# A wait at the shared port: GpSimd's port operations wait by semaphore for the VectorE operation that the plan put ahead of them

## The chip, the cores and the metric

The kernel runs on one core of one Trainium2 chip. The metric is the device time of one launch in microseconds (us), lower is better. Before the change three runs took 1005.16, 1011.17 and 1012.47 us (median 1011.17).

## The reference, cut to what matters

The reference is a two-layer encoder trunk on 256 tokens of width 1024, all in float32. Each layer is a SwiGLU FFN (width 2816), a mixer, and a second SwiGLU FFN, each between two RMS norms:

```
x = x + 0.5 * rmsnorm(swiglu(rmsnorm(x, g0), wg0, wu0, wd0), g1)
m = mixer(rmsnorm(x, g2));  x = x + rmsnorm(m, g3)
x = x + 0.5 * rmsnorm(swiglu(rmsnorm(x, g4), wg1, wu1, wd1), g5)
```

The mixer of layer 0 (the even mixer) projects to nine parts, turns queries and keys by rotary tables (RoPE), runs four differential attention heads and eight heads whose keys are selected by an indexer (the 64 best keys of each query), and projects the result back. The mixer of layer 1 is a chunked band attention with a relative bias. Only the even mixer has work for GpSimd at the port that this change is about.

## The kernel before, in words

**Tiling.** Tokens stand in two tiles of 128 rows. Every product of two float32 matrices is made of three products of rounded parts: a tile is split into a high part (a cast) and a low part (the tile less the high part), and TensorE adds high by high, high by low and low by high. For weights this is done by `Unit.start` (from L250 on): SyncE loads a 512 KB piece of the weights into a staging buffer `raw` (L269, 6 such buffers), ScalarE casts it to `wh` (L277) in pieces of 128x512, and the low part `wl` is one subtraction per piece (L279, `lo`), which reads `raw` and `wh`, both in SBUF. There are 8 buffers each for `wh` and `wl`.

**Which engine makes the low parts.** In the FFNs and in layer 1 it is VectorE (DVE). In the even mixer the units `ua[1]` to `ua[5]` and `uo` are made with `pool=True`: the subtraction may then go to VectorE or to GpSimd (POOL), to whichever the plan finds free first. The same holds for the sum at the end of `rope` (L744): a tile `t` plus a tile `t`, both in SBUF, of 512 or 288 columns. What `rope` does ahead of it (L736, L740) reads PSUM and stays on VectorE. The transposes of a rope's result on TensorE are L427.

**The plan sets the order.** All operations are first written into a list (`Plan.op`), with an estimated duration, a place in the order (`pos`) and the operations that they depend on. `Plan.issue` (L93) then runs a small event simulation with one clock per engine, and calls each operation's function when the simulated engine takes it; that fixes the order of the instructions on every engine. On the chip each engine works through its own row in order, and waits by semaphores for data and buffers alone.

**The port in the plan.** Operations that are marked `port=True` are held to use one port that VectorE and GpSimd share: while one of them runs in the simulation (until `port`, set when it is taken), no other marked operation of the two engines is taken. Nothing of this reaches the chip: there, the two engines meet at the port as their own waits let them.

Of the kernel before, what the change touches and what calls it, by code (L numbers as in the profile page):

```python
# [52 lines left out]
class Plan:  # L53
# [36 lines left out]
        self.pos += us  # L90
        return self.last

    def issue(self):  # L93
        free = dict(SLOTS)
        eng = {e: 0.6 for e in LAT}
        heap = {e: [] for e in LAT}
        ev, n, port = [], 0, 0.0
        todo = len(self.ops)

        def push(o):  # L100
            for e in o["eng"]:
                heapq.heappush(heap[e], (o["pos"], o["id"], o))

        def event(t, kind, x):
            nonlocal n
            n += 1
            heapq.heappush(ev, (t, n, kind, x))

        for o in self.ops:
            if o["n"] == 0:  # L110
                push(o)
        event(0.6, "", None)
        now = 0.0
        while ev:
            now = ev[0][0]
            while ev and ev[0][0] <= now + 1e-9:
                _, _, kind, x = heapq.heappop(ev)
                if kind == "ready":
                    push(x)
                elif kind == "free":  # L120
                    free[x.tag] += x.n
            for e in heap:
                if eng[e] > now + 1e-9:
                    continue
                skip, got, late = [], None, None
                while heap[e]:
                    z = heapq.heappop(heap[e])
                    o = z[2]
                    if o["end"] is not None:
                        continue  # L130
                    need = [q for q in o["refs"] if q.t is None]
                    fits = all(free[q.tag] >= sum(p.n for p in need if p.tag == q.tag) for q in need)

                    if o["port"] and e != "ACT" and port > now + 1e-9:
                        fits = False
                        event(port, "", None)
                    for q in o["refs"]:

                        if q.tag in BANKS and q.used[0] != e and q.used[1] > now + 1e-9:
                            fits = False  # L140
                            event(q.used[1], "", None)
                    if fits and o["safe"] <= now + 1e-9:
                        got = o
                        break
                    if fits and late is None:
                        late = z
                    skip.append(z)
                if got is None and late is not None:
                    got = late[2]
                    skip.remove(late)  # L150
                for z in skip:
                    heapq.heappush(heap[e], z)
                if got is None:
                    continue
                o = got
                need = [q for q in o["refs"] if q.t is None]
                for q in need:
                    free[q.tag] -= q.n
                    q.t = q.make()
                us = o["us"] if len(o["eng"]) == 1 else o["us"][e]  # L160
                o["fn"]() if len(o["eng"]) == 1 else o["fn"](e)
                if o["port"] and e != "ACT":
                    port = now + us
                end = eng[e] = o["end"] = now + us
                todo -= 1
                event(end, "", None)
                for q in o["refs"]:
                    q.used = (e, end + 0.1)
                for d in o["out"]:
                    d["n"] -= 1  # L170
                    at = end + (OWN[e] if d["eng"] == (e,) else o["lat"])
                    d["ready"] = max(d["ready"], at)
                    if d["eng"] == ("PE",) != (e,):
                        d["safe"] = max(d["safe"], at + SAFE)
                    if d["n"] == 0:
                        d["ready"] = max(d["ready"], now)
                        event(d["ready"], "ready", d)
                for q in o["refs"]:
                    q.left -= 1
                    if q.left == 0:  # L180
                        event(end + 0.05, "free", q)
        assert todo == 0, [(o["eng"], o["pos"], o["n"], [q.tag for q in o["refs"]])
                           for o in self.ops if o["end"] is None][:20]
        return now
# [11 lines left out]
def trunk_kernel(  # L196
# [25 lines left out]
    pl = Plan()  # L222
    op, main = pl.op, pl.main
    PE, ACT, DVE, POOL, DMA = ("PE",), ("ACT",), ("DVE",), ("POOL",), ("DMA",)
# [895 lines left out]
    for l in range(2):  # L1120
        for p in range(3):
# [11 lines left out]
            else:  # L1133
                ffn(l, p // 2, xT, nxt)
            xT = z
    pl.issue()


# [48 lines left out]
```

## Time and profile before

| what | value |
| --- | --- |
| median of three runs | 1011.17 us |
| the three runs | 1005.16, 1011.17, 1012.47 us |
| the profiled execution, time | 1006.86 us |
| its span on the core | 1005.1 us |
| busy in the span: TensorE (PE) | 991.6 us, 99% |
| busy: VectorE (DVE) | 725.7 us, 72% |
| busy: ScalarE (ACT) | 607.4 us, 60% |
| busy: GpSimd (POOL) | 85.2 us, 8%, 107 instructions |
| TensorE's granted clock, mean | 0.999 of full speed |

The profile is one execution, so its rows add up to its own span of 1005.1 us, and some 1.8 us lie around it in the 1006.86 us. Rows of a timeline give the start from the span's beginning, the time of one or of several merged instructions (x5 is five of them), the engine, the line of the kernel, and in square brackets how long the engine had been idle and what ended it. An instruction that stands at the port is shown as busy: it has started, and lasts longer.

### The profile page before, as it was taken

How to read it: one execution, taken by the hardware profiler on the slowest of the kernel's cores; microseconds unless marked ns; L12 is line 12 of the kernel's file. 1: busy time of each engine (PE TensorE's matmuls, PEld its weight loads, DVE VectorE, ACT ScalarE, POOL GpSimd, SP SyncE). 2: the span in 40 equal slices, each digit the busy share in tenths (PEclk: the TensorE clock that was granted, in tenths of full speed). 3: DMA queues.
4: the chain of work that ended last, by engine and by line, in shares of the span. 5: the costliest groups of instructions: out<-in, count | busy, mean ns of one | idle time of the engine just before them, and what ended most of it. 6: DMA issues, size and time to landing. Idle time of an engine off the chain costs nothing.

```text
span 1005.1 us, 15484 instructions
## 1 busy us (share of the span) xinstructions
PE 991.6 (99%) x5435; PEld 847.6 (84%) x5435; DVE 725.7 (72%) x1537; ACT 607.4 (60%) x1376; POOL 85.2 (8%) x107
## 2 busy tenths in 40 slices
PE   9999999999999999999999999999999999999997
PEld 8888888877888988888888888888888888888886
DVE  7766668689888676677577667676778877666682
ACT  8555556556588555565466555576578856555661
POOL 1000000156531100000020000001100010000000
PEclk9999999999999999999999999999999999999999
DMA  9866665555545567666467666664775447666621
GB/s 343 293 184 178 196 191 144 161 178 167 167 138 157 166 218 200 192 187 190 146 209 247 180 182 192 195 178 149 224 267 159 124 148 251 188 179 194 192 87 42
DMA packets 125933, 185.52 MB, mean 185 GB/s; under 512 B 6040, under 2 KB 93984, under 8 KB 125856
## 3 DMA queue, kind: packets, MB, share of 16 engines
q1 hardware_dynamic: 125856, 184.54, 59.9%
q8 instruction: 42, 0.69, 0.3%
q14 instruction: 35, 0.29, 0.1%
HBM read 183.47 MB, written 1.05 MB: 184 GB/s over the span
## 4 chain that ended last, share of the span: by engine, by line
PE 89%; DVE 7%; ACT 2%; issue 1%; DMA 1%; POOLq 0%; DVEq 0%; ACTq 0%; POOL 0%
PE ps L387 26%; PE ps L389 14%; PE y L417 9%; PE y L418 9%; PE y L419 9%; PE ps L412 4%; PE ps L409 4%; PE ps L410 4%; PE ps L427 2%; DVE wl L279 2%; PE ps L417 2%; PE ps L418 2%; PE ps L419 2%; PE ps L795 1%; DMA g<-in_norm_g_dram 1%
## 5 line engine op out<-in xcount | busy, mean ns | idle before, releaser
L279 DVE TENSOR_TENSOR wl<-raw,wh 128x512 fp32r<-128x512 f32 (+2 forms) x636 | 418.0, 689 | 133.5 <-ACT wh L277 91.3
L277 ACT CAST wh<-raw 128x512 fp32r<-128x512 f32 (+2 forms) x668 | 378.8, 615 | 124.5 <-issue 70.1
L387 PE MATMUL ps<-xT,wh 128*128 128x512 f32 x1152 | 290.4, 393 | 0.0
L387 PEld LDWEIGHTS ps<-xT,wh 128*128 128x128 f32 x1152 | 208.1, 189 | 38.0
L389 PEld LDWEIGHTS ps<-xT,wl 128*128 128x128 f32 x1152 | 157.5, 190 | 11.6
L389 PE MATMUL ps<-xT,wl 128*128 128x256 f32 x1152 | 162.8, 283 | 0.0
L417 PE MATMUL y<-wh,blk 128*128 128x512 f32 x352 | 138.1, 392 | 0.0
L418 PE MATMUL y<-wl,blk 128*128 128x512 f32 x352 | 137.4, 390 | 0.0
L419 PE MATMUL y<-wh,blk 128*128 128x512 f32 x352 | 137.1, 390 | 0.0
L409 PE MATMUL ps<-wh,xT 128*128 128x512 f32 (+2 forms) x320 | 107.6, 351 | 0.1
L410 PE MATMUL ps<-wl,xT 128*128 128x512 f32 (+2 forms) x320 | 106.1, 347 | 0.8 <-DVE wl L279 0.3
L396 DVE TENSOR_TENSOR t<-ps,t 128x256 f32<-128x256 f32 x144 | 60.6, 421 | 44.3 <-ACT t L395 42.8
L395 ACT COPY t<-ps 128x256 f32<-128x256 f32 x144 | 53.6, 373 | 51.8 <-PE ps L389 48.0
L453 POOL TENSOR_TENSOR sm<-sm 128x1 f32<-128x1 f32 x24 | 14.9, 621 | 777.9 <-ACT t L534 721.4
L419 PEld LDWEIGHTS y<-wh,blk 128*128 128x128 f32 x352 | 66.1, 188 | 13.9
L417 PEld LDWEIGHTS y<-wh,blk 128*128 128x128 f32 x352 | 66.2, 188 | 12.8
L418 PEld LDWEIGHTS y<-wl,blk 128*128 128x128 f32 x352 | 66.2, 188 | 12.6
L410 PEld LDWEIGHTS ps<-wl,xT 128*128 128x128 f32 x320 | 60.6, 189 | 8.8 <-DVE wl L279 2.3
L412 PE MATMUL ps<-wh,xT 128*128 128x512 f32 (+2 forms) x320 | 67.6, 347 | 0.0
L409 PEld LDWEIGHTS ps<-wh,xT 128*128 128x128 f32 x320 | 60.5, 189 | 8.0 <-ACT xT L363 0.5
L680 ACT ACTIVATE t<-t 128x256 f32<-128x256 f32 x64 | 26.8, 418 | 55.2 <-DVE t L679 55.2
L412 PEld LDWEIGHTS ps<-wh,xT 128*128 128x128 f32 x320 | 51.3, 189 | 6.6
(148 smaller groups left out, 1030.7 us busy)
## 6 DMA issues: line engine op xcount, KB each, us to landing
raw<-in_wd_dram SPq DMA_DIRECT2D x88, 512.0 KB, 4.2
raw<-in_wg_dram SPq DMA_DIRECT2D x86, 512.0 KB, 4.4
raw<-in_wu_dram SPq DMA_DIRECT2D x86, 512.0 KB, 4.5
raw<-in_ew_in_dram SPq DMA_DIRECT2D x24, 512.0 KB, 4.6
raw<-in_ow_in_dram SPq DMA_DIRECT2D x24, 512.0 KB, 4.5
g<-in_norm_g_dram SPq DMA_DIRECT2D x11, 512.0 KB, 5.7
raw<-in_ew_out_dram SPq DMA_DIRECT2D x8, 512.0 KB, 3.7
raw<-in_ow_out_dram SPq DMA_DIRECT2D x8, 512.0 KB, 4.0
```

The source lines that it names most:

```text
L277: nc.scalar.copy(ref.t[0][:, sl], raw.t[:, sl])
L279: (nc.vector if e == "DVE" else nc.gpsimd).tensor_sub(ref.t[1][:, sl], raw.t[:, sl], ref.t[0][:, sl].bitcast(F32))
L387: nc.tensor.matmul(b.t, w()[0], xT.both[:, k].rearrange("p j c -> p (j c)"), start=k == 0, stop=False)
L389: nc.tensor.matmul(b.t[:, 0:S], w()[1], xT.t[0][:, k, :], start=False, stop=k == KT - 1)
L395: op(ACT, n_act(S, True), lambda: nc.scalar.copy(dst.t[:, sl], b.t[:, S:512]), r=[b], w=[(dst, sl.start)])
L396: op(DVE, n_dve(S), lambda: nc.vector.tensor_add(dst.t[:, sl], b.t[:, 0:S], dst.t[:, sl]), r=[b], w=[(dst, sl.start)])
L409: nc.tensor.matmul(o(), ah, bh, start=k == 0, stop=False)
L410: nc.tensor.matmul(o(), ah, bl, start=False, stop=False)
L412: nc.tensor.matmul(o(), al, bh, start=False, stop=k == KT - 1)
L417: nc.tensor.matmul(o, ah, bh, start=start, stop=False)
L418: nc.tensor.matmul(o, ah, bl, start=False, stop=False)
L419: nc.tensor.matmul(o, al, bh, start=False, stop=stop)
```

## The change

`issue` now gets the tile context `tc`. In the simulation it remembers in `held` the last VectorE operation that was taken at the port, and to each GpSimd operation taken at the port it adds a dependency on that one, of the kind that becomes a semaphore wait on the chip. The wait goes one way: VectorE's operations get none for GpSimd's.

```diff
-    def issue(self):
+    def issue(self, tc):
...
-        ev, n, port = [], 0, 0.0
+        ev, n, port, held = [], 0, 0.0, None
...
                 if o["port"] and e != "ACT":
                     port = now + us
+
+                    done = tc.nc.cur_bb.bb.instructions[-1]
+                    if e == "DVE":
+                        held = done
+                    elif held is not None:
+                        tc.add_manual_dep(done, held.name, mybir.DependencyInfo(mybir.DependencyClass.Sync, mybir.DependencyReason.DATA),
+                                          reason="port")
...
-    pl.issue()
+    pl.issue(tc)
```

The order of the instructions stays the same on all five engines; what changes is what some of them wait for. The first two pieces are GpSimd's row in the even mixer, from its second rope sum on: `t` are the two tiles of that sum, `wl`, `wh` and `raw` the low part, the high part and the staging buffer of a weight piece, and the names in brackets are the semaphores waited for. Before:

```order
27 L744 TENSOR_TENSOR t_360_2196<-t_360_2196,t_361_2202 128x512 [waits DVE_49,PE_49]
28 L279 TENSOR_TENSOR wl_2225<-raw_2036,wh_2224 128x512 [waits DMAHW0_49,Activation_49]
29 L279 TENSOR_TENSOR wl_2252<-raw_2084,wh_2251 128x512 [waits DMAHW3_49,PE_49,Activation_49]
30 L279 TENSOR_TENSOR wl_2263<-raw_2129,wh_2262 128x512 [waits DMAHW5_49,PE_49,Activation_49]
31 L744 TENSOR_TENSOR t_370_2240<-t_370_2240,t_371_2245 128x288 [waits DVE_49]
32 L894 COPY t_370_2240<-t_370_2240 128x96 [waits Pool_49]
33 L279 TENSOR_TENSOR wl_2319<-raw_2275,wh_2318 128x512 [waits DMAHW1_49,Activation_49]
```

And GpSimd's row at the same place with the change (its lines are seven further down in the file):

```order
27 L751 TENSOR_TENSOR t_360_2196<-t_360_2196,t_361_2202 128x512 [waits DVE_49,PE_49]
28 L286 TENSOR_TENSOR wl_2225<-raw_2036,wh_2224 128x512 [waits DMAHW0_49,Activation_49]
29 L286 TENSOR_TENSOR wl_2252<-raw_2084,wh_2251 128x512 [waits DVE_49,DMAHW3_49,PE_49,Activation_49]
30 L286 TENSOR_TENSOR wl_2263<-raw_2129,wh_2262 128x512 [waits DMAHW5_49,PE_49,Activation_49]
31 L751 TENSOR_TENSOR t_370_2240<-t_370_2240,t_371_2245 128x288
32 L901 COPY t_370_2240<-t_370_2240 128x96 [waits Pool_49]
33 L286 TENSOR_TENSOR wl_2319<-raw_2275,wh_2318 128x512 [waits DMAHW1_49,DVE_49,Activation_49]
```

Two subtractions (29 and 33) have gained a wait for VectorE; the sum in 31 has lost its own, which the wait in 29 covers, since GpSimd works in order. The sum in 27 names the same semaphore as before, but the value waited for is higher by one instruction: it stands for the second multiplication of L529 now, and for the rope's L740 before. Of GpSimd's 32 subtractions nine have gained a wait in this way: each is the first of a run of GpSimd operations that follows port work on VectorE in the plan.

SyncE's row changes too. The pieces below are its loads of staging buffers at the time of those GpSimd operations. Before:

```order
98 L269 DMA raw_2312<-in_ew_in_dram 128x2x512 [waits DMAHW3_49,DVE_49,Pool_49]
99 L269 DMA raw_2328<-in_ew_in_dram 128x2x512 [waits DMAHW4_49,DMAHW5_49,DVE_49,Pool_49]
100 L269 DMA raw_2360<-in_ew_in_dram 128x2x512 [waits DMAHW7_49,DVE_49]
101 L269 DMA raw_2375<-in_ew_in_dram 128x2x512 [waits DMAHW1_49,DMAHW6_49,Activation_49,Pool_49]
102 L269 DMA raw_2430<-in_ew_in_dram 128x2x512 [waits DMAHW0_49,DVE_49]
```

With the change the same five loads read:

```order
98 L276 DMA raw_2312<-in_ew_in_dram 128x2x512 [waits DMAHW3_49,Pool_49]
99 L276 DMA raw_2328<-in_ew_in_dram 128x2x512 [waits DMAHW4_49,DMAHW5_49,DVE_49,Pool_49]
100 L276 DMA raw_2360<-in_ew_in_dram 128x2x512 [waits DMAHW7_49,DVE_49]
101 L276 DMA raw_2375<-in_ew_in_dram 128x2x512 [waits DMAHW6_49,DMAHW0_49,DVE_49]
102 L276 DMA raw_2430<-in_ew_in_dram 128x2x512 [waits DMAHW1_49,Activation_49,Pool_49]
```

The loads 101 and 102 have changed staging buffers: the buffer that GpSimd frees is now taken by the later of the two, the one that VectorE frees by the earlier.

## Rows read from the trace of the kernel before

**Rows 1.** The page's first part: busy time of the engines in the whole span, share of the span, instructions.
```profile
PE 991.6 (99%) x5435; PEld 847.6 (84%) x5435; DVE 725.7 (72%) x1537; ACT 607.4 (60%) x1376; POOL 85.2 (8%) x107
```

**Rows 2.** Busy time by stretch of the span (us from its start): length, then busy us of each engine with its instructions, granted clock, share of the DMA engines, GB/s.
```profile
0.00:10.00 10.00, 8.29 (x38) 6.82 (x38) 4.52 (x17) 6.18 (x19) 0.69 (x6) 1.00 0.77 244
...
200.00:310.00 110.00, 105.86 (x639) 86.25 (x638) 96.54 (x272) 72.50 (x193) 53.83 (x43) 1.00 0.51 157
310.00:995.00 685.00, 684.06 (x3732) 588.00 (x3732) 487.94 (x985) 412.31 (x913) 23.11 (x42) 1.00 0.60 183
995.00:1005.07 10.07, 3.57 (x16) 2.63 (x14) 3.00 (x6) 1.38 (x4) 0.74 (x2) 0.87 0.15 53
```

**Rows 3.** The same view, two pieces of 10 us out of the even mixer.
```profile
210.00:220.00 10.00, 9.48 (x44) 7.20 (x42) 9.97 (x15) 7.33 (x14) 8.72 (x8) 1.00 0.52 143
220.00:230.00 10.00, 7.81 (x55) 6.06 (x55) 9.82 (x16) 3.21 (x9) 2.85 (x3) 1.00 0.64 219
```

**Rows 4.** Waits of TensorE's matmuls between 200 and 310 us: who waited for whom, us in total, times, the longest.
```profile
PE ps L427 <- DVE t L744: 2.5, 2, 1.7
PE ps L427 <- DVE pt L369: 0.7, 1, 0.7
PE ps L427 <- POOL t L744: 0.5, 1, 0.5
```

**Rows 5.** Timeline of TensorE, pieces between 210 and 231 us.
```profile
210.84 0.66 PE L427 MATMUL ps<-ident,t 128*128 128x128 f32 x4 [0.52 <-POOL t L744]
...
213.64 1.98 PE L412 MATMUL ps<-wh,xT 128*128 128x512 f32 x8
...
219.51 0.49 PE L427 MATMUL ps<-ident,t 128*128 128x128 f32 x3
221.67 0.63 PE L427 MATMUL ps<-ident,t 128*128 128x128 f32 x4 [1.67 <-DVE t L744]
...
230.35 0.63 PE L427 MATMUL ps<-ident,t 128*128 128x128 f32 x4 [0.87 <-DVE t L744]
```

**Rows 6.** Timeline of GpSimd between 203 and 224 us.
```profile
204.37 0.81 POOL L744 TENSOR_TENSOR t<-t,t 128x288 f32<-128x288 f32 x1 [2.05 <-DVE t L740]
...
209.19 1.60 POOL L744 TENSOR_TENSOR t<-t,t 128x512 f32<-128x512 f32 x1 [3.69 <-DVE t L740]
210.75 1.29 POOL L279 TENSOR_TENSOR wl<-raw,wh 128x512 fp32r<-128x512 f32 x1
212.72 3.32 POOL L279 TENSOR_TENSOR wl<-raw,wh 128x512 fp32r<-128x512 f32 x2 [0.68 <-ACT wh L277]
216.00 1.24 POOL L744 TENSOR_TENSOR t<-t,t 128x288 f32<-128x288 f32 x1
217.31 0.61 POOL L894 COPY t<-t 128x96 f32<-128x96 f32 x1
217.89 1.29 POOL L279 TENSOR_TENSOR wl<-raw,wh 128x512 fp32r<-128x512 f32 x1
219.71 2.94 POOL L279 TENSOR_TENSOR wl<-raw,wh 128x512 fp32r<-128x512 f32 x2 [0.54 <-ACT wh L277]
```

**Rows 7.** Timeline of VectorE, pieces between 208 and 231 us.
```profile
208.17 0.87 DVE L740 SCALAR_TENSOR_TENSOR t<-ps,sm,r 128x256 f32<-128x256 f32 x2
208.96 0.68 DVE L529 TENSOR_TENSOR blk<-X,g 128x512 f32<-128x512 f32 x1
...
211.13 6.67 DVE L279 TENSOR_TENSOR wl<-raw,wh 128x512 fp32r<-128x512 f32 x5
217.72 0.68 DVE L371 SCALAR_TENSOR_TENSOR blk<-ps,blk 128x512 fp32r<-128x512 f32 x1
218.32 0.73 DVE L736 SCALAR_TENSOR_TENSOR t<-ps,sm,r 128x512 f32<-128x512 f32 x1
218.98 0.86 DVE L740 SCALAR_TENSOR_TENSOR t<-ps,sm,r 128x256 f32<-128x256 f32 x2
219.88 1.65 DVE L744 TENSOR_TENSOR t<-t,t 128x512 f32<-128x512 f32 x1
221.45 3.56 DVE L279 TENSOR_TENSOR wl<-raw,wh 128x512 fp32r<-128x512 f32 x4
...
229.52 0.69 DVE L744 TENSOR_TENSOR t<-t,t 128x512 f32<-128x512 f32 x1
```

**Rows 8.** Groups of instructions: VectorE's subtractions between 200 and 310 us; the columns are line, engine, operation, tiles, shapes, count, then busy us, mean ns of one, idle us ahead of them with what ended it.
```profile
L279 DVE TENSOR_TENSOR wl<-raw,wh 128x512 fp32r<-128x512 f32 x27 | 23.1, 896 | 2.4 <-ACT wh L277 2.3
```

**Rows 9.** The same group between 310 and 990 us, where GpSimd makes no low parts.
```profile
L279 DVE TENSOR_TENSOR wl<-raw,wh 128x512 fp32r<-128x512 f32 x458 | 300.2, 686 | 100.2 <-ACT wh L277 68.3 <-PE ps L389 30.9
```

**Rows 10.** GpSimd's instructions that write or read `wl`: duration in ns, shortest, median and longest, first and last start in us.
```profile
L279 POOL TENSOR_TENSOR wl<-raw,wh x32: 1264/1292/2551, 210.7 to 302.2; 128x512 fp32r<-128x512 f32 x32
```

**Rows 11.** Timelines at two later places: GpSimd's subtractions at 261 and 284 us.
```profile
261.09 2.55 POOL L279 TENSOR_TENSOR wl<-raw,wh 128x512 fp32r<-128x512 f32 x1 [4.95 <-ACT wh L277]
...
284.14 1.76 POOL L279 TENSOR_TENSOR wl<-raw,wh 128x512 fp32r<-128x512 f32 x1 [1.14 <-ACT wh L277]
```

**Rows 12.** VectorE at the same two places.
```profile
260.61 0.69 DVE L744 TENSOR_TENSOR t<-t,t 128x512 f32<-128x512 f32 x1
261.21 1.29 DVE L279 TENSOR_TENSOR wl<-raw,wh 128x512 fp32r<-128x512 f32 x2
...
283.47 3.58 DVE L279 TENSOR_TENSOR wl<-raw,wh 128x512 fp32r<-128x512 f32 x4
```

## The prediction

> **What bounds the kernel now.** The first view is the busy time of the engines: TensorE is busy 991.6 of 1005.1 us, GpSimd 85.2 [rows 1]. The kernel's time is TensorE's work plus the 13.5 us in which it stands. The second view, busy time by stretch, says where it stands: 1.7 us in the first 10 us, 6.5 us in the last 10, 0.9 us in the 685 us from 310 on, and 110.00 - 105.86 = 4.14 us between 200 and 310 us [rows 2]. That is the even mixer, the only place where GpSimd makes low parts. No edit at the port can give back more than these 4.14 us, unless TensorE's own work got shorter, and the change leaves its instructions and their order as they are.
>
> The third view names what TensorE waits for there: 2.5 us in two waits for VectorE's rope sums and 0.5 us in one wait for GpSimd's rope sum [rows 4]; the timeline puts them at 210.84 (0.52 us), 221.67 (1.67 us) and 230.35 (0.87 us) [rows 5]. VectorE is busy 9.97 and 9.82 of 10 us just there [rows 3], but part of that is standing at the port. A subtraction takes it 686 ns where GpSimd is quiet [rows 9] and 896 ns on average between 200 and 310 us [rows 8]; 27 x 0.21 = 5.7 us are lost so. It can be seen in single rows: from 211.13 five subtractions take 6.67 us, while GpSimd works beside them, and the rope sum at 219.88 takes 1.65 us, while GpSimd runs two subtractions from 219.71 [rows 6, 7]. At 261 two of VectorE's subtractions with no GpSimd operation ahead of them take 1.29 us, a step of 0.60 us each and 0.69 for the last [rows 12].
>
> GpSimd stands as well: its subtractions take 1.29 us in the median and 2.55 us at the longest [rows 10]. Where one stands, it ends a fixed time after the other's operation: VectorE's run of five ends at 217.80, which is 0.56 us after GpSimd's sum ended (216.00 + 1.24) [rows 6, 7]; GpSimd's sum of 209.19 ends at 210.79, 1.15 us after VectorE's L529 ended (208.96 + 0.68).
>
> On the first of these I weighed a rule of the Trainium skill. SBUF — State Buffer, "Who interferes with whom", says that a VectorE operation with two SBUF inputs and a GpSimd operation that reads SBUF exclude each other for a whole instruction, and that whoever issues first gets the port. The rows at 211 to 218 us agree. Those at 261 do not agree in the second half: GpSimd's subtraction started at 261.09, yet the two of VectorE that followed, from 261.21 on, went ahead unstretched, and GpSimd ended at 263.64 [rows 11, 12]. By the rule the port's total time stays what it is and a wait only chooses who stands; what that gives is the first rival below.
>
> **The change part by part.** It adds nine waits to GpSimd's subtractions and raises the value of one that a rope sum already had. No instruction is added to VectorE, TensorE or ScalarE. A wait matters only where the named VectorE operation ends after GpSimd would have started.
>
> *First place, 209 us.* GpSimd's rope sum (27 in its order) must now wait for L529, which ends at 209.64. It already stood for it at the port and ended at 210.79 [rows 6, 7]. Semaphore to start is 0.15 us (L740 ended at 209.04, the sum started at 209.19), a clean operation 1.29 us: it would end at 209.64 + 0.15 + 1.29 = 211.08. TensorE waits for it at 210.84 already [rows 5], so this costs 0.3 us.
>
> *Second place, 212 us.* Subtraction 29 started at 212.72; now it waits for the last of VectorE's five subtractions, which ended at 217.80: 5.08 us late if nothing else moved. But VectorE's run gets shorter. Its first still stands behind GpSimd's 28 (ends 212.04, plus 0.56 = 212.60), the other four take 0.60 each: 215.00, which is 2.8 us earlier. GpSimd then starts at 215.15 and its two subtractions end at 215.15 + 2 x 1.29 = 217.73, where they ended at 216.04. VectorE meanwhile does L371, L736 and L740, which read PSUM; L736 needs TensorE's products, done at 213.64 + 1.98 = 215.62 [rows 5], so its rope sum L744 is asked for at 215.66 + 0.66 + 0.80 = 217.1, stands until 217.73, and ends at 218.3 in place of 221.53. GpSimd's small sum (31; 0.81 us clean [rows 6]) comes behind it and ends at 218.3 + 0.66 = 219.0, the copy (32; 0.26 to 0.61) at 219.2 to 219.6. Queued behind the wait are thus 30, 31 and 32, and TensorE waits for 32 at 219.51 [rows 5]: 0 to 0.2 us late. The next transposes, which stood 1.67 us for L744, stand no more. Gain: 1.67 - 0.2 = 1.5 us.
>
> *Third place, 218 us.* Subtraction 33 (started 217.89) now waits for VectorE's four subtractions from 221.45. These come after L744 and GpSimd's small sum, the first ending near 219.5, the last near 221.3 (before: 225.01). GpSimd's three then run from 221.45 to 225.3, where they ended at 222.65. They are 2.7 us late. No wait of TensorE for a GpSimd low part is among [rows 4]; what waits for them is SyncE, for a staging buffer. There the exchange of buffers helps: load 101 no longer waits for GpSimd, load 102 does. I cost this at nothing; the cover is the slack of loads and casts ahead of the products, and without it the price is 2.7 us. That is below the second rival's and does not come on top of it: a TensorE that is late at the second place wants these parts later by as much.
>
> *Fourth place, 230 us.* TensorE stands 0.87 us for VectorE's L744 of 229.52. VectorE's backlog ahead of it has become 3.7 us shorter (225.01 against 221.3), TensorE's products that feed L736 come 1.2 us earlier. The wait can go fully or not at all; I take half, 0.4 us.
>
> *The others.* At 261 GpSimd stood until VectorE was done (2.55 us instead of 1.29), so the wait only makes standing into waiting: 0. At 284 it will start 1.3 us later and VectorE's run of four (3.58 us; clean 3 x 0.60 + 0.69 = 2.5) gets 1.1 us shorter [rows 11, 12]; no wait of TensorE in [rows 4] is for either: 0.
>
> *Sum:* +0.3 - 1.5 - 0.4 = -1.6 us. Ends: -4.1 us if every wait of TensorE in this stretch goes, +3.1 us if the second place turns against TensorE (second rival). I take the sum, since its largest term rests on a single row that shows both the stretch and the wait. What is late next after L744 is the copy 32. The profiled execution took 1006.86 us, so it would take 1005.3; it lies 4.3 us below the median of the three runs, and on that the forecast is 1011.17 - 1.6 = 1009.6 us.
>
> **The rivals.**
>
> *The port's time is only shared out anew.* VectorE gets no wait for GpSimd, so GpSimd's late operations meet later VectorE operations, as L744 at the second place does. Then VectorE's 5.7 us come back elsewhere, TensorE's waits move, and the net is the 0.3 us of the first place: 1011.5 us. For it: the longest stretches are not all covered by a wait (VectorE's first subtraction at 211.13 stays behind GpSimd's 28, which has none). Against it: between 221 and 231 us VectorE works on PSUM for the most part, where GpSimd costs it nothing, as L371, L736 and L740 of 217.72 to 219.84 show, at 0.43 to 0.73 us each beside a busy GpSimd [rows 6, 7]. The rule of the Trainium skill's page SBUF — State Buffer, named above, is for this rival.
>
> *Slower: GpSimd's late copy makes TensorE stand.* Place: the transposes at 219.51. They have 2.26 us after the end of the small sum at 217.24, and 1.6 us after that of the copy (217.92). If VectorE's five subtractions do not get shorter, GpSimd is released at 217.80, 5.08 us late; by the slack of the small sum 5.08 - 2.26 = 2.8 us reach TensorE, and with the first place's 0.3 it is +3.1: 1014.3 us. It decides from the point at which VectorE's run ends after 216.6 (215.0 plus the copy's slack). For it: VectorE's run depends on casts of ScalarE too. Against it: VectorE shows no idle between 211.13 and 219.88.
>
> *The change does not do what it says.* The waits are there in GpSimd's order, but one-way; if at the port VectorE mostly goes ahead anyway, as at 261, they say only what happens already: 0, that is 1011.2 us.
>
> **How the numbers follow.** The forecast (a gain of 1 to 4 us) gets 0.50, sharing anew 0.22, no effect 0.10, slower by 1 us or more 0.18. All four lie within 1% (10 us), which is about what a measurement of this kernel can tell from no change: the three runs already span 7.3 us. Beyond 1% on either side there is only the spread of runs or a mechanism that I don't see: 0.04 each, 0.92 for the same. The range takes the ends on the lowest and the highest run: 1005.16 - 4.1 = 1001.0 and 1012.47 + 3.1 = 1015.6. The forecast's own is 1007 to 1010.
>
> **What would show it.** Right: VectorE's five subtractions at 211 take near 3.9 us (212.60 - 211.13 = 1.5, and 4 x 0.60) and its L744 behind them 0.7 to 1.2; the wait of 1.67 us is gone; GpSimd waits for VectorE near 213 and 219 us; TensorE's busy time between 200 and 310 us nearer to the stretch's length. Wrong: a wait of TensorE for GpSimd's copy or sum of over 1 us, VectorE's mean in rows 8 still near 896 ns, or TensorE waiting for casts whose load stood behind GpSimd.

## The result, and the profile after

The change takes 1003.73 us (median of 7 runs, 1001.74 to 1005.65); the kernel before, run beside it, 1009.98 us (7 runs, 1005.16 to 1012.47). The ratio is 0.9943, with a 95% interval from 0.9920 to 0.9966: 0.57% faster, 6.25 us between the medians. The prediction was 1009.6 us and a gain of 1.6 us: inside 1%, as most of its chance said, and inside the wide range of 1001.0 to 1015.6, but below the forecast's own 1007 to 1010 us, and the gain is four times as large.

The profiled execution of the change took 1003.96 us, its span is 1002.2 us, 2.9 us shorter than that of before. First the busy times of the whole span:

```profile
PE 991.6 (99%) x5435; PEld 847.9 (85%) x5435; DVE 721.9 (72%) x1537; ACT 607.4 (61%) x1376; POOL 82.5 (8%) x107
```

TensorE has the same work as in [rows 1]. VectorE and GpSimd are "busy" 3.8 and 2.7 us less with the same instructions: that was standing at the port. In the timelines and groups below a line of the kernel stands seven further down than before (L279 is L286, L744 is L751, L427 is L434). The stretch from 200 to 310 us, columns as in [rows 2]:

```profile
200.00:310.00 110.00, 108.39 (x652) 88.61 (x651) 94.84 (x279) 75.18 (x200) 50.28 (x43) 1.00 0.51 161
```

TensorE stands 110.00 - 108.39 = 1.61 us there, against 4.14. Its waits in this stretch, to set beside [rows 4]:

```profile
PE ps L434 <- DVE pt L376: 0.7, 1, 0.7
PE ps L434 <- POOL t L751: 0.6, 1, 0.6
PE ps L802 <- DVE blk L378: 0.3, 1, 0.3
```

The two waits for VectorE's rope sums, 2.5 us, are gone. The columns are who waited for whom, us in total, times and the longest, as there. Now GpSimd's timeline, to set beside [rows 6]:

```profile
209.55 1.29 POOL L751 TENSOR_TENSOR t<-t,t 128x512 f32<-128x512 f32 x1 [4.07 <-DMA raw<-in_ew_in_dram]
210.79 1.30 POOL L286 TENSOR_TENSOR wl<-raw,wh 128x512 fp32r<-128x512 f32 x1
215.27 2.55 POOL L286 TENSOR_TENSOR wl<-raw,wh 128x512 fp32r<-128x512 f32 x2 [3.18 <-PE ps L419]
217.77 1.27 POOL L751 TENSOR_TENSOR t<-t,t 128x288 f32<-128x288 f32 x1
219.10 0.61 POOL L901 COPY t<-t 128x96 f32<-128x96 f32 x1
221.59 3.79 POOL L286 TENSOR_TENSOR wl<-raw,wh 128x512 fp32r<-128x512 f32 x3 [1.88 <-ACT blk L372]
```

And VectorE's operations that meet it, to set beside [rows 7]:

```profile
210.90 4.14 DVE L286 TENSOR_TENSOR wl<-raw,wh 128x512 fp32r<-128x512 f32 x5
...
217.27 1.10 DVE L751 TENSOR_TENSOR t<-t,t 128x512 f32<-128x512 f32 x1
218.29 3.16 DVE L286 TENSOR_TENSOR wl<-raw,wh 128x512 fp32r<-128x512 f32 x4
...
225.97 0.68 DVE L751 TENSOR_TENSOR t<-t,t 128x512 f32<-128x512 f32 x1
```

GpSimd starts its pair at 215.27, 0.23 us after VectorE's five end (210.90 + 4.14 = 215.04), and its three at 221.59, 0.14 us after the four end (218.29 + 3.16 = 221.45). The releasers printed there, PE and ACT, are only the last semaphore event that the profile sees; the ends of VectorE's rows tell what was waited for. VectorE's five take 4.14 us in place of 6.67, the four 3.16 in place of 3.56, and its second rope sum comes at 225.97 in place of 229.52. GpSimd's pair starts 2.55 us late and its three end at 225.38 in place of 222.65, and no wait of TensorE for a low part of GpSimd appears. In the same group between 200 and 310 us the mean of a subtraction on VectorE falls from the 896 ns of [rows 8] to

```profile
L286 DVE TENSOR_TENSOR wl<-raw,wh 128x512 fp32r<-128x512 f32 x28 | 19.8, 745 | 2.4 <-ACT wh L284 2.3
```

Between these two profiled executions the gain is 2.9 us, 2.5 of them in this stretch. The other 3.4 us of the 6.25 are the question that the experiments answer.

### The profile page after: what moved, and what is told of

The parts are those of the page before. It is cut to its first block, busy times and chain, and to the rows that moved or that the text cites. A ratio compares the mean times of both kernels' runs of the same rounds, so it can differ in the third digit from the quotient of the medians.

```text
span 1002.2 us, 15484 instructions
## 1 busy us (share of the span) xinstructions
PE 991.6 (99%) x5435; PEld 847.9 (85%) x5435; DVE 721.9 (72%) x1537; ACT 607.4 (61%) x1376; POOL 82.5 (8%) x107
## 4 chain that ended last, share of the span: by engine, by line
PE 92%; DVE 4%; ACT 1%; DMA 1%; issue 1%; SPq 0%; POOL 0%; POOLq 0%; DVEq 0%; ACTq 0%
PE ps L394 26%; PE ps L396 14%; PE y L424 9%; PE y L425 9%; PE y L426 9%; PE ps L416 5%; PE ps L419 5%; PE ps L417 5%; PE ps L434 3%; PE ps L426 2%; PE ps L425 2%; PE ps L424 2%; PE ps L802 1%; DVE wl L286 1%; DMA g<-in_norm_g_dram 1%
## 5 line engine op out<-in xcount | busy, mean ns | idle before, releaser
L286 DVE TENSOR_TENSOR wl<-raw,wh 128x512 fp32r<-128x512 f32 (+2 forms) x636 | 414.1, 683 | 133.8 <-ACT wh L284 89.7
```

The source lines that it names most:

```text
L286: (nc.vector if e == "DVE" else nc.gpsimd).tensor_sub(ref.t[1][:, sl], raw.t[:, sl], ref.t[0][:, sl].bitcast(F32))
```

## The experiments

All runs below were taken in three groups; the median of before in them is 1009.5 (23 runs), 1009.01 (23) and 1008.64 us (18). Ratios are to the kernel before, in the same group, with 95% intervals. In the edits `nth` counts GpSimd's port operations in the plan's order; the line that counts them is not shown, and it moves the later lines of the kernel down by one more (L279 is L287, L744 is L752, L427 is L435).

### What does before usually look like? (again, again2: the kernel before, unchanged)

> The kernel before once more, nothing changed, for a second profiled execution and more times. Theory A (lottery at the port): without the waits the order at the port is settled anew in each execution by small shifts, so executions of the same program stand differently long in the even mixer; the times spread from 1005 to 1012 us with a median near 1010, and in the new profile TensorE stands for another time between 200 and 310 us than the 4.14 us of the first profile, while the stretches outside agree within 0.5 us. Theory B (elsewhere): what lies between the first profile (1006.86 us) and the median (1009.98) is loading or start-up, so TensorE stands for 4.1 us again between 200 and 310 us and the difference shows in other stretches. Theory C (chance): the true time of before is near 1006.9 us and the gain is the 2.9 us of the two profiles; the median here is then 1007 us or less.

1009.84 us (1005.38 to 1011.31, 12 runs), ratio 1.0000 (0.9987 to 1.0014). The profiled execution took 1010.72 us, with a span of 1008.7 us, 3.6 more than the profile that the prediction was made from. Its page, the first line:

```profile
PE 993.0 (98%) x5435; PEld 848.4 (84%) x5435; DVE 728.5 (72%) x1537; ACT 607.7 (60%) x1376; POOL 87.2 (9%) x107
```

TensorE's same work takes 1.4 us more than in [rows 1]. The stretch:

```profile
200.00:310.00 110.00, 103.75 (x612) 84.03 (x610) 96.00 (x260) 70.31 (x186) 54.91 (x43) 0.98 0.50 156
```

TensorE stands 6.25 us there and not 4.14, and its granted clock is 0.98 in the mean. 2.1 + 1.4 = 3.5 us: that is the difference of 3.6 us but for 0.1 us. TensorE's timeline shows the place; compare the last line of [rows 5]:

```profile
232.67 1.09 PE L427 MATMUL ps<-ident,t 128*128 128x128 f32 x4 [3.96 <-DVE t L744]
233.41 2.05 PE L412 MATMUL ps<-wh,xT 128*128 128x512 f32 x4
```

It stands 3.96 us for the rope sum for which it stood 0.87 us in the first profile. The granted clock, the third figure from the end, in the 2 us in which the stand ends (at 232.67), and in the 2 after these:

```profile
232.00:234.00 2.00, 1.33 (x6) 1.27 (x7) 1.83 (x5) 0.21 (x1) 1.65 (x1) 0.50 0.88 255
234.00:236.00 2.00, 2.00 (x24) 1.25 (x26) 1.46 (x6) 1.41 (x3) 0.00 (x0) 0.64 0.57 139
```

0.50 is the lower of the two levels, 1.2 GHz: four transposes take 1.09 us in place of 0.63. The reason for the stand is on VectorE:

```profile
220.65 4.68 DVE L279 TENSOR_TENSOR wl<-raw,wh 128x512 fp32r<-128x512 f32 x4
...
229.23 1.62 DVE L279 TENSOR_TENSOR wl<-raw,wh 128x512 fp32r<-128x512 f32 x1
230.78 1.75 DVE L744 TENSOR_TENSOR t<-t,t 128x512 f32<-128x512 f32 x1
```

and GpSimd:

```profile
220.72 3.45 POOL L279 TENSOR_TENSOR wl<-raw,wh 128x512 fp32r<-128x512 f32 x2 [1.38 <-ACT wh L277]
229.04 4.62 POOL L279 TENSOR_TENSOR wl<-raw,wh 128x512 fp32r<-128x512 f32 x3 [4.87 <-ACT wh L277]
```

VectorE's four take 4.68 us in place of 3.56, because GpSimd's two lie wholly beside them. Then GpSimd's three start at 229.04, just ahead of VectorE's last subtraction and its rope sum; each of these loses a turn (it stands until an operation of GpSimd has ended), and the two together take 3.30 us (229.23 to 232.53). In the profile of [rows 7] the rope sum took 0.69 us, for GpSimd came when both had started, 0.29 us behind the sum's start at 229.52:

```profile
228.92 0.68 DVE L279 TENSOR_TENSOR wl<-raw,wh 128x512 fp32r<-128x512 f32 x1
...
229.81 4.04 POOL L279 TENSOR_TENSOR wl<-raw,wh 128x512 fp32r<-128x512 f32 x3 [7.15 <-ACT wh L277]
```

> The kernel before once more, unchanged, for a third profiled execution. Theory A: if its time is 1009 us or more, TensorE stands 2 us or more for VectorE's rope sum near 230 us, GpSimd's subtraction there has started ahead of VectorE's pair, and the granted clock falls below 1.00 in the 4 us behind the stand; if it is 1007 us or less, the stand there is about 1 us and the clock holds.

1009.13 us in one run. Again a single large stand, and the same rows on VectorE:

```profile
218.84 4.67 DVE L279 TENSOR_TENSOR wl<-raw,wh 128x512 fp32r<-128x512 f32 x4
...
227.42 1.59 DVE L279 TENSOR_TENSOR wl<-raw,wh 128x512 fp32r<-128x512 f32 x1
228.94 1.74 DVE L744 TENSOR_TENSOR t<-t,t 128x512 f32<-128x512 f32 x1
```

```profile
230.83 1.08 PE L427 MATMUL ps<-ident,t 128*128 128x128 f32 x4 [3.95 <-DVE t L744]
```

TensorE stands 3.95 us for this sum and works at a granted clock of 0.50 from 232 to 234 us. So two of three profiled executions of before, both near the median, lose at 230 us what the third, near the shortest of its runs, does not.

### Which of the waits gives the gain? Halves first (early, late)

```diff
-                    elif held is not None:
+                    elif held is not None and nth <= 9:    # early; late: nth > 9
```

Early keeps the waits up to 223 us (the prediction's places one to three), late those from 230 us on.

> The waits of the change only for the first nine GpSimd operations at the port (those up to 223 us); the other 28 go without, as before. My step in the prediction: the whole gain comes from the second and fourth places, both shaped by these waits, so nearly all of the gain is here: 1003.5 to 1005 us, TensorE's waits for VectorE's rope sums (1.67 and 0.87 us) gone in the profile. Theory A with the lottery spread over the whole even mixer: only half of the 6.2 us is here, 1006 to 1007 us, and the times spread more than those of the change (1001.7 to 1005.7).

1003.09 us (1001.87 to 1005.11, 6 runs), ratio 0.9938 (0.9920 to 0.9955): all of the gain.

> The complement: the first nine GpSimd operations at the port go without the added wait, the other 28 have it. My step: no gain from these, the time of before, 1009 to 1011 us, with TensorE's wait of 1.67 us near 221 us still there. Theory A with the lottery spread over the whole even mixer: half of the gain, 1006 to 1007 us.

1006.73 us (1004.72 to 1009.84, 12 runs), ratio 0.9975 (0.9961 to 0.9988): nearly half of it. In its profile, the longest of its executions (1009.84 us), VectorE's pair at 230 us is clean (0.68 and 0.68), the four still take 4.68, and TensorE stands 1.97 us for the sum.

### Place by place (place2, place3, place4)

```diff
-                    elif held is not None:
+                    elif held is not None and nth <= 6:          # place2: places one and two
+                    elif held is not None and 7 <= nth <= 9:     # place3: subtraction 33 alone
+                    elif held is not None and nth == 10:         # place4: the subtraction of 230 us alone
```

Each kernel has one of the three lines.

> Only the waits of the first and second places (the rope sum at 209 us behind the second L529, and the subtraction at 212 us behind VectorE's five); no wait from 217 us on. Theory A as the runs so far shape it: an execution of before stands 1 to 2 us near 221 and then 1 to 4 us near 230 us, and where it stands 2 us or more there TensorE's granted clock falls behind it. By the prediction's step, VectorE's five take 4.1 us in place of 6.7, so the first of the two stands goes, but GpSimd's next three subtractions meet VectorE's four again, and part of the second stand stays: 1005 to 1006.5 us. Rival (one wait does all: VectorE, once 2.5 us ahead, keeps ahead): 1003 to 1004 us as with all waits.

1006.41 us (1004.34 to 1009.86, 12 runs), ratio 0.9982 (0.9970 to 0.9995). At the second place all is as in the change: the five take 4.13, the sum behind them 1.10, and the stand at 221 is gone. Then GpSimd's three meet VectorE's four:

```profile
218.41 5.35 DVE L287 TENSOR_TENSOR wl<-raw,wh 128x512 fp32r<-128x512 f32 x4
...
228.27 1.76 DVE L752 TENSOR_TENSOR t<-t,t 128x512 f32<-128x512 f32 x1
```

and TensorE still stands 2.33 us for the last sum:

```profile
230.17 0.63 PE L435 MATMUL ps<-ident,t 128*128 128x128 f32 x4 [2.33 <-DVE t L752]
```

> Only the wait of the third place (the subtraction at 218 us behind VectorE's four), which the prediction cost at nothing. Theory A: the five at 211 us still take 6.7 us and TensorE stands about 0.7 us near 221, but the four after it take 2.5 to 3.2 us in place of 3.6 to 4.7, VectorE has 1.5 to 2 us more ahead of 230 us, and most of the second stand goes: 1004.5 to 1006 us. Rival (the prediction's cost of this place was right): no gain, 1009 to 1010 us.

1003.12 us (1001.70 to 1004.29, 6 runs), ratio 0.9949 (0.9932 to 0.9967). The gain is larger than I had expected of this place (1004.5 to 1006 us): one semaphore wait gives what all ten edited waits give. VectorE in its profile:

```profile
210.65 4.71 DVE L287 TENSOR_TENSOR wl<-raw,wh 128x512 fp32r<-128x512 f32 x5
...
217.43 0.72 DVE L752 TENSOR_TENSOR t<-t,t 128x512 f32<-128x512 f32 x1
218.07 2.48 DVE L287 TENSOR_TENSOR wl<-raw,wh 128x512 fp32r<-128x512 f32 x4
...
224.80 0.68 DVE L287 TENSOR_TENSOR wl<-raw,wh 128x512 fp32r<-128x512 f32 x1
225.40 0.69 DVE L752 TENSOR_TENSOR t<-t,t 128x512 f32<-128x512 f32 x1
```

TensorE's transposes for that sum follow without a stand:

```profile
227.01 0.60 PE L435 MATMUL ps<-ident,t 128*128 128x128 f32 x4
```

GpSimd:

```profile
220.69 3.78 POOL L287 TENSOR_TENSOR wl<-raw,wh 128x512 fp32r<-128x512 f32 x3 [3.09 <-ACT blk L373]
...
227.50 3.81 POOL L287 TENSOR_TENSOR wl<-raw,wh 128x512 fp32r<-128x512 f32 x3 [3.02 <-ACT wh L285]
```

The wait lets the four run clean (2.48 us). VectorE then is done with its pair (225.40 + 0.69 = 226.09) 1.4 us before GpSimd wants the port at 227.50, so the pair is clean too, with no wait for it; the only stand of TensorE that its waits still list in the stretch is 0.3 us. One thing in this profile is not the wait's doing: the five took 4.71 us (4.47 in place3b), where I had expected 6.7 and again2 has 5.90, and no wait was put ahead of what they meet. Five of 5.90 us would have ended the pair up to 1.2 us later, at 227.3, and left TensorE a stand of at most some 0.4 us (an estimate from these rows).

> Only the wait of the fourth place (the subtraction at 230 us behind VectorE's subtraction and rope sum there). The run with all waits from 230 us on took 1006.7 us. Theory A: this one wait is what it lived on, since it keeps GpSimd's subtraction from starting just ahead of VectorE's pair, which then takes 3.3 us in place of 1.3: 1006 to 1007.5 us, the stand near 230 us never above 2 us. Rival (the later waits, at 246, 261, 284 us, give their share): 1008 to 1009.5 us.

1005.51 us (1004.04 to 1007.80, 12 runs), ratio 0.9971 (0.9959 to 0.9982). The pair is clean, the four still take 4.67, and TensorE stands 1.96 us:

```profile
218.60 4.67 DVE L287 TENSOR_TENSOR wl<-raw,wh 128x512 fp32r<-128x512 f32 x4
...
227.78 0.69 DVE L752 TENSOR_TENSOR t<-t,t 128x512 f32<-128x512 f32 x1
...
228.61 0.63 PE L435 MATMUL ps<-ident,t 128*128 128x128 f32 x4 [1.96 <-DVE t L752]
```

These runs take again2's stand of 3.95 us apart, each by one profiled execution. A clean pair is worth 1.59 + 1.74 - 0.68 - 0.69 = 1.96 us: place4 keeps 1.96 of the stand. Four clean subtractions are worth 4.67 - 2.48 = 2.19 us, and they bring the clean pair with them: place3 keeps nothing (of which up to 0.4 us may be the five's). The gains of places two, three and four (0.18, 0.51, 0.29%) add up to 0.98%, and the change has 0.57%: they are cuts at one and the same stand.

### All but the third place (not3)

```diff
-                    elif held is not None:
+                    elif held is not None and not 7 <= nth <= 9:
```

> All waits of the change but the one of the third place. Alone, the third took 1003.1 us, the second 1006.4, the fourth 1005.5 us, before 1009 us. Theory A as it stands now: TensorE's long stand near 230 us is VectorE's lateness there, made up of about 2.2 us from its four subtractions near 219 us and 2.1 us from its pair near 228 us, where each stands behind GpSimd's three; without the third wait the four stay at 4.7 to 5.4 us and the pair becomes clean: a stand of 0.5 to 2 us near 230 us and 1004.5 to 1006 us. Rival (any one early wait is enough, once the pair at 228 us is safe too): 1003 to 1004 us, as the change.

1004.35 us (1003.53 to 1007.35, 7 runs), ratio 0.9965 (0.9950 to 0.9981). The four take 5.36, as in place2, but the pair is clean, and of the stand 1.10 us is left, with the granted clock at 1.00 from 226 to 236 us:

```profile
217.11 5.36 DVE L287 TENSOR_TENSOR wl<-raw,wh 128x512 fp32r<-128x512 f32 x4
...
227.81 0.63 PE L435 MATMUL ps<-ident,t 128*128 128x128 f32 x4 [1.10 <-DVE t L752]
```

So the third wait is enough alone, but the others can do most of its work; whether it adds anything to them the intervals don't tell (change2, in the same group, has 0.9937 to 0.9972). The exchange of the staging buffers, which the change brings too, was not tried alone. Nothing in the profiles points to it: in every profile of before the stands that go are for VectorE's rope sums, and no matmul of TensorE between 200 and 310 us waits for a cast or a low part, before or after.

### Is the port's time only shared out anew? (twoway)

Here VectorE's port operations also wait, for the GpSimd operation ahead of them in the plan.

```diff
-        ev, n, port, held = [], 0, 0.0, None
+        ev, n, port, held = [], 0, 0.0, {}
...
-                    if e == "DVE":
-                        held = done
-                    elif held is not None:
-                        tc.add_manual_dep(done, held.name, mybir.DependencyInfo(
...
+                    held[e] = done
+                    ahead = held.get("POOL" if e == "DVE" else "DVE")
+                    if ahead is not None:
+                        tc.add_manual_dep(done, ahead.name, mybir.DependencyInfo(
...
```

> The change, and the same wait the other way: each VectorE operation at the port also waits for the GpSimd operation that the plan put ahead of it, so that the two never meet at the port. If what is left of meetings costs time (VectorE's first subtraction of five at 211 and its rope sum at 217 still stand 0.9 and 0.4 us in the profile of the change), this is 0.5 to 1.5 us faster than the change: 1002 to 1003 us. If the order of the plan fits the chip badly, VectorE, busy over 9 of 10 us there, now waits for a GpSimd that is late, with PSUM work queued behind the wait: 1005 to 1010 us. I take the second as likelier, since the wait also stops the work behind that does not touch the port.

1003.44 us (1002.24 to 1004.64, 6 runs), ratio 0.9939 (0.9921 to 0.9956), the same as the change. I had expected it to be slower, and it is not. VectorE's five take 3.10 us and the four 2.56, all clean, but VectorE waits for GpSimd, 1.11 us ahead of the five and 1.52 us ahead of the rope sum: standing became waiting, and the remaining stretches (4.14 and 3.16 in the change) cost TensorE nothing.

### How much of the loss is the clock? (fill)

The kernel before, with 14 matmuls of the identity by itself put ahead of the transposes that stand at 230 us; what they write is overwritten by the transposes.

```diff
-    def transposes(src, rk, nblk, pos=None):
+    def transposes(src, rk, nblk, pos=None, fill=0):
...
+            for _ in range(fill):
+                nc.tensor.matmul(b.t[:, 0:P], ident.t, ident.t, start=True, stop=True)
...
-            proj_rope(ua[1], xT, t, KB, None)
+            proj_rope(ua[1], xT, t, KB, None, fill=0 if t else 14)
```

> The kernel before, with 14 extra 128x128 matmuls put ahead of the transposes near 230 us for which TensorE stands (they multiply the identity by itself into the bank that the transposes then write; nothing else reads them). TensorE is thus busy for some 3 us of the stand. VectorE and GpSimd are not touched, so the stand's end does not move. Theory A: the part of the loss that is the granted clock (0.83 between 226 and 236 us after a stand of 2 to 4 us; some 1.2 us by the stretched transposes and products behind it) goes, and the port's part stays: 1007.5 to 1008.5 us, granted clock 0.95 or more between 226 and 236 us. Rival (the clock costs nothing of its own): 1009 us or more, since the extra matmuls take time where the stand is short.

1006.75 us (1006.24 to 1008.70, 12 runs), ratio 0.9986 (0.9975 to 0.9997). On TensorE, where the 14 matmuls (now L427; the transposes are L429) appear as 28:

```profile
226.69 3.29 PE L427 MATMUL ps<-ident 128*128 128x128 f32 x28
230.73 0.66 PE L429 MATMUL ps<-ident,t 128*128 128x128 f32 x4 [0.75 <-DVE t L746]
231.14 1.17 PE L412 MATMUL ps<-wh,xT 128*128 128x512 f32 x4
```

The transposes start at 230.73, in again2 at 230.83: the port is as bad as before (four 4.67, pair 1.63 and 1.75), and of the stand 0.75 us is left empty. But the granted clock stays at 1.00, and the four products behind the transposes take 1.17 in place of 2.05 us. With no change at the port 1.9 us by the medians come back (0.3 to 2.5 by the interval): that is the clock's part in a usual execution of before. The shortest runs are gone as well: even its shortest, 1006.24, is above before's shortest of 1005.31.

### The change and the single wait once more (change2, place3b)

> The change once more, unchanged, beside the next run on one chip: 1003 to 1004 us, the reference for whether the one wait of the third place alone is faster than all.

> The wait of the third place alone once more, unchanged. If the other waits are idle once this one is there: the same as the change, 1003 to 1004 us, within 0.5 us of it. If the raised wait of the first place costs the 0.3 us that the prediction gave it: 0.3 us faster.

1004.01 us (1001.85 to 1005.21, 6 runs), ratio 0.9955 (0.9937 to 0.9972), and 1003.65 us (1002.31 to 1004.44, 6 runs), ratio 0.9952 (0.9936 to 0.9968). The two can't be told apart, and neither can early, twoway and the change; no kernel of these beats the change by a measurable amount. In the profile of change2 TensorE waits 0.97 us for GpSimd's rope sum at the first place, in that of place3b not at all.

## Why the prediction was right and where it was wrong

**What bounds the kernel** was right: TensorE's work, plus its standing between 200 and 310 us. The cap was wrong. "No edit at the port can give back more than these 4.14 us" was read from one execution. In the other two profiled ones TensorE stands 5.0 to 6.25 us there, and works 0.9 to 1.4 us longer at a lower clock (992.5 and 993.0 us busy). The exclusion "unless TensorE's own work got shorter" is just what occurred. The gain of 6.25 us lies above this cap, and above the 1 to 4 us that the forecast called its own.

**First place** (+0.3): the order of the operations came as described (GpSimd's sum starts 0.14 us after the multiplication of L529, now L536, ends, and takes its clean 1.29 us); the price was not shown. With this wait TensorE stands 0.58 us there in the change, 0.97 in change2, 0.72 in place2, and not at all in early, not3 and twoway; without it 0.52 in before, 0.53 in again and not at all in again2.

**Second place** (-1.5): right for the execution that it was read from. Forecast were 3.9 us for the five, 0.7 to 1.2 for the sum behind them, its end at 218.3, the copy's end at 219.2 to 219.6; measured 4.14, 1.10, 218.37 and 219.71. The stand of 1.67 us went. TensorE's matmuls don't wait for the copy, one of its weight loads does, for 0.25 us; the text had 0 to 0.2. But the 1.67 us were a matter of luck: the same stand is 0.72 us in again and missing in again2, so what the wait of this place gives there (0.18% in place2) seems to lie mostly at the fourth place, where TensorE stands 2.33 in place of 3.95 us.

**Third place** (0): this is the term that was mis-sized most. I asked only whether GpSimd's low parts would come too late, and that was answered rightly: they come late and nobody waits. What the wait does for VectorE got no price here. The four at a clean step of 0.60 us are in the text, in the 221.3 at which the last of them ends, but they were counted only into the fourth place's backlog, and that was given 0.4 us. In the executions that lose at 230 us the four go from 4.67 to 2.48 us, with a rope sum that TensorE waits for behind them. It could have been asked of the rows: the four of [rows 7] took 3.56 us against the clean 2.5, and stood 8 us ahead of that rope sum. Alone, this wait is worth 0.51%, the whole gain within the intervals.

**Fourth place** (-0.4, a half of 0.87): the stand went fully. The text had the reason, a backlog shorter by 3.7 us (221.45 against 225.01: 3.56, and the rope sum 3.55 earlier), and still took half. In again and again2 the stand is not 0.87 but 3.96 and 3.95 us.

**The sum and its base.** -1.6 us against 2.9 between the two profiles. The base came out 1.2 us lower with seven runs than with three (1009.98 against 1011.17). The larger miss is the shift onto the median: taking 1.6 from 1011.17 supposes that the 4.3 us between the profiled execution and the median lie where the change can't reach. In again 3.5 us of them are in this very stretch: 2.1 us of standing (3.1 more at the fourth place, 1.0 less at the second, where the sum's stand was 0.72) and 1.4 us of slowed work. The change takes them away as well. That the time came out within 1% owes more to the width of the forecast than to its sum.

**The rivals.** *Shared out anew*: not here; the stretched operations that are left cost TensorE nothing, and the two-way order is no faster. The rule of the Trainium skill that stood for this rival (SBUF — State Buffer, "Who interferes with whom": one engine at a time, and a whole instruction at a time) is borne out by the lost turns (0.69 us becomes 1.75), but the total that the prediction took from it as fixed need not fall on the path: twoway's waits of 1.11 and 1.52 us don't. *Slower by GpSimd's late copy*: no, the five got shorter and ended 1.6 us before the point named. *No effect*: no.

## What to carry to other kernels

Where two engines meet at a shared port, price an added order from both engines' side: what the waiting one is late for, and what the other one now reaches earlier, down to the next thing that the bounding engine waits for. Where the runs of a kernel lie some us apart, its profile shows one of them: ask what in that execution came out by luck (here, which of two engines reached the port first) before its waits are taken as the most that can be gained. Gains at places that feed one stand are not added.

## What the runs showed of the hardware

- One lost turn at the port costs an operation of VectorE of this size some 1.07 us (0.69 to 1.76), and where both engines run back to back most operations lose one (five took 6.67 in place of 3.10 us, which is some three turns; four 5.35 in place of 2.48, some 2.7); operations of VectorE that read PSUM lose none (L736 of [rows 7] takes its 0.73 us beside GpSimd's subtraction of 217.89).
- A stand of TensorE of 1.96 to 3.96 us (late, place2, place4, again, again2) was each time followed by a granted clock of 0.50 to 0.53 in one of the 2 us pieces in the 4 us behind it; stands of 0.87, 1.10 and 1.67 us (before, not3) were not: 1.00 throughout. With the stand filled by matmuls the clock stayed at 1.00. Why some stands are followed by it and others not, these runs don't settle.
- Left open: by which rule the port lets GpSimd wait through two operations of VectorE at 261 us [rows 11, 12] and alternates at 229 us; no run here forced either order. Nor was it shown that the spread of before's runs is this alone: the three profiles agree with it, the other runs have only their times.
